# Gate and up projections of a hybrid decoder layer: from feature-major tiles to token-major 2x2 block products with seven products in place of eight

## The chip, the cores and the metric

The kernel runs on one core of one Trainium2 chip. The metric is device time in microseconds (us) of one execution. Before the change the median of three runs is 1140.72 us (1139.92 to 1142.09).

## The reference, cut to what matters

One decoder layer in float32, 256 tokens, model width 2048, feed-forward width 5632. The part that changes is the SwiGLU; the first residual, its norm and the down projection stand next to it.

```python
h = h + jnp.einsum('bse,ed->bsd', y, w_out[l])
u = rmsnorm(h, ln2_w[l])
ff = jax.nn.silu(jnp.einsum('bsd,df->bsf', u, w_ffn_gate[l])) * jnp.einsum('bsd,df->bsf', u, w_ffn_up[l])
h = h + jnp.einsum('bsf,fd->bsd', ff, w_ffn_down[l])
```

## The kernel before

Every large product is made of operands split into a high and a low part (`split`, L90: ScalarE copies the value to a rounded type, VectorE subtracts that copy from the value); high x high, high x low and low x high are summed in PSUM. Weights come from HBM in units of 128 x 2048 (class `Unit`, L94), two halves of 512 KB each, each issued on SyncE's queue into a `raw` tile (four slots) and split into `wh` and `wl` tiles (four slots each).

The work is a list, `program`, of steps: each has the unit it needs and a function that issues its matmuls. The loop at the end runs through it and issues loads three halves ahead of the step (`AHEAD`); `defer` puts work off by a number of steps. A planner orders the instructions of each engine's queue by this order and by when they are ready; each engine works its queue in order.

Two layouts occur. Feature-major (`fm_tile`, L151, `mm_fm`, L128): a 128-column tile of weights is the stationary operand, and the activations of all 256 tokens, high and low part side by side, are the moving one: 512 columns against the weights' high part and 256 against the low part, for each of 16 contraction tiles. Token-major (`tm_block`, L166, `mm_tm`, L139): 128 tokens are the stationary operand and 512 columns of weights the moving one, three matmuls for each contraction tile.

The gate and up projections are feature-major: 44 tiles of gate and 44 of up in turn, 88 steps. Behind each pair `ffn_post` (L545) adds the halves of the PSUM banks (`halves`, L146), applies the norm's scale, the tanh and the products, on VectorE, ScalarE and, for one multiplication, GpSimd (L551), and splits the result into `ff`, already in the layout that the down projection takes as stationary operand. The down projection is token-major. Before them stands the output projection, whose `out_post` (L502) adds the residual and makes the split left operands `hh`, 16 tiles. `resid_tok` (L532) transposes the residual on TensorE (L536) during the gate and up projections.

Other lines that are spoken of: L442 and L443 (`head`, attention scores, matmuls on whole float32 operands), L480 and L484 (`group_norm_apply`, GpSimd), L378 to L383 (`lru_out`, VectorE and ScalarE), L84 (matmuls at the start that warm TensorE up), L574 (`down_post`, VectorE reads PSUM).

Of the kernel before, what the change touches and what calls it, by code (L numbers as in the profile page):

```python
# [25 lines left out]
# columns of the packed per-channel parameters  # L26
# [5 lines left out]
def tile_hymba_layer(ctx: ExitStack, tc: tile.TileContext, A: dict, out: bass.AP):  # L32
# [48 lines left out]
    # the tensor engine's clock rises while the first loads are under way  # L81
# [12 lines left out]
    class Unit:  # L94
        """[128, 2048] of weights in two halves: 16 tiles of 128 columns, or 4 of 512."""
# [23 lines left out]
        def part(self, k, w, c0, cw):  # L119
            """columns c0:c0+cw of the k-th tile of width w, both parts"""  # L120
            o = k * w + c0
            j, o = o // 1024, o % 1024
            return self.h[j][:, o : o + cw], self.l[j][:, o : o + cw]

    halfway = []  # work to put into the middle of the next feature-major tile
    program = []  # (units to have loaded, compute)

    def mm_fm(ps, wh, wl, hl, first, last):  # L128
        """feature-major: ps[:, :256] + ps[:, 256:] collects w.T @ a"""
        pe.matmul(ps, wh, hl, start=first, stop=False)  # L130
        pe.matmul(ps[:, :S], wl, hl[:, :S], start=False, stop=last)  # L131

    def mm_fm1(ps, wh, wl, hl, first, last):
        """feature-major: ps collects w.T @ a"""
# [4 lines left out]
    def mm_tm(ps, hl, t, wh, wl, first, last):  # L139
        """token-major: ps collects a[:, tokens of t].T @ w"""  # L140
        ah, al = hl[:, t * P : t * P + P], hl[:, S + t * P : S + t * P + P]
# [4 lines left out]
    def halves(ps, dst):  # L146
        """dst = ps[:, :256] + ps[:, 256:]"""
# [18 lines left out]
    def tm_block(units, acts, post, together=1, split=()):  # L166
        """the last `together` units make one step, token tile after token tile; the last token
        tile's columns may be cut into pieces, each with a bank of its own"""
# [3 lines left out]
        def mm(unit, i, k, piece):  # L172
# [3 lines left out]
            mm_tm(ps[piece][:, c0 : c0 + cw], acts[4 * i + k], t, wh, wl, first, last)  # L176
# [25 lines left out]
    # work put off by a number of program steps  # L202
# [16 lines left out]
    def rsqrt_small(dst, var, scale, n):  # L219
        """dst = 1 / sqrt(var * scale + EPS), one Newton step behind the table's root"""  # L220
# [5 lines left out]
        # r (1.5 - 0.5 v r^2)  # L226
# [5 lines left out]
    def rms_scale(sumsq, r_tok, r_bc, then=None):  # L232
        """sumsq [128, 256]: squares summed over the tiles, not yet over the partitions"""
# [22 lines left out]
    r2 = cpool.tile([P, S], F32, name="r2")  # L256
    sumsq = cpool.tile([P, 512], F32, name="sumsq")

# [24 lines left out]
    xc = [None] * 4  # convolved input, two channel tiles each  # L283
    tt = [None] * 4  # tanh(c r / 2)
# [15 lines left out]
    def lru_decay():  # L300
        """c2 = -4 log_sigmoid(lambda) = 4 (log1p(exp(-|l|)) + max(-l, 0))"""
# [4 lines left out]
        # exp(-w) = (1 - tanh(w/2)) / (1 + tanh(w/2)) at w = |l| / 8, then three squarings  # L306
# [6 lines left out]
        # log1p(z) = 2 atanh(z / (2 + z))  # L313
# [46 lines left out]
    def lru_scan(n):  # L360
        """a = (1-T)/(1+T), sqrt(1-a^2) = (s^2 + T) / (s (1+T)) with s = sqrt(T) and a Heron step"""
# [32 lines left out]
    vv = [None] * 4  # [t][block]  # L394
# [91 lines left out]
    def ret_y(h):  # L486
# [5 lines left out]
        g = gnh[:, h : h + 1]  # half of the weight: sg is twice the gate  # L492
# [7 lines left out]
    hh = [None] * KT  # L500

    def out_post(f, ps):  # L502
        x = xs(f)
        if f < KT - 2:
            t = tmp("op")
            halves(ps, t)
            v.tensor_tensor(out=x, in0=x, in1=t, op=ALU.add)
        else:
            v.tensor_tensor(out=x, in0=ps[:, :S], in1=x, op=ALU.add)
        hl = act_tile("h", F32R)  # L510
        act.activation(out=hl[:, :S], in_=x, func=AF.Copy, scale=col(C_LN2 + f))
        v.scalar_tensor_tensor(
            out=hl[:, S:], in0=x, scalar=col(C_LN2 + f), in1=hl[:, :S].bitcast(F32),
            op0=ALU.mult, op1=ALU.subtract,
        )
        hh[f] = hl
        sq = sumsq[:, :S] if f == 0 else tmp("sq")
# [4 lines left out]
    r2h = cpool.tile([P, S], F32, name="r2h")  # L522

    def norm2():
        def half():
            v.tensor_scalar(out=r2h, in0=r2, scalar1=0.5, scalar2=None, op0=ALU.mult)

        rms_scale(sumsq[:, :S], r2_tok, r2, half)
# [3 lines left out]
    def resid_tok(cb):  # L532
        ps = [aux("ht"), aux("ht")]
        for i in range(4):
            for t in range(2):
                pe.transpose(ps[t][:, i * P : i * P + P], xs(4 * cb + i)[:, t * P : t * P + P], ident)  # L536
        for t in range(2):
            htok[(cb, t)] = xpool.tile([P, 512], F32, tag="xh", name=nm("htok"))
            act.copy(out=htok[(cb, t)], in_=ps[t])

# [1 line left out]
    ff = [None] * FT  # L542
    gate_ps = {}

    def ffn_post(f, gps, ups):  # L545
        g, s, w = tmp("fg"), tmp("fs"), tmp("fu")
        halves(gps, g)
# [289 lines left out]
```

## Time and profile before

| | |
|---|---|
| median of the runs | 1140.72 us (1139.92 to 1142.09) |
| the profiled execution | span 1138.9 us; the median of the runs is 1.8 us more |
| TensorE, weight loads, VectorE | busy 1119.9, 981.6, 744.2 us |
| ScalarE, GpSimd | busy 567.5, 111.4 us |
| DMA | 214.86 MB, mean 189 GB/s |

The span runs from the first to the last instruction of the profiled execution. Matmuls are pipelined: their recorded durations overlap, so the distance from one start to the next is what one costs. PE is TensorE, PEld its weight loads, DVE VectorE, ACT ScalarE, POOL GpSimd, SP SyncE.

### The profile page before, as it was taken

Reading aid. Unit: us, or ns where it says so; the run is one execution under the profiler, and the core shown is the slowest. Engines: PE = TensorE matmul, PEld = TensorE weight load, DVE = VectorE, ACT = ScalarE, POOL = GpSimd, SP = SyncE. Lnnn points to the kernel's source line nnn. Section 1 sums busy time; section 2 is a strip of 40 time slices with the busy share of each in tenths; the row PEclk is TensorE's granted clock in tenths of the full one; section 3 lists DMA queues with packets and bytes.
Section 4 is the critical chain, followed back from the end, with each engine's and each line's share of the span. In section 5 each row is a group of like instructions: output and inputs, shape, how many; then the busy total and the mean of one; then the engine's idle time right before and its main releaser. Section 6 shows DMA issues by size and latency. Waiting matters only on the chain.

```text
span 1138.9 us, 16705 instructions
## 1 busy us (share of the span) xinstructions
PE 1119.9 (98%) x6418; PEld 981.6 (86%) x6418; DVE 744.2 (65%) x1092; ACT 567.5 (50%) x826; POOL 111.4 (10%) x126
## 2 busy tenths in 40 slices
PE   7999999999999999999999999999999999999996
PEld 7998888889888988888888888888888888888896
DVE  7797899658877666666666666666666544444544
ACT  7575544456555555455554445445444434343432
POOL 4022310004400000000000000000000000000100
PEclk9999999999999999999999999999999999999999
DMA  7755655645455566555556555655655665656652
GB/s 244 250 167 174 229 172 184 204 148 183 151 185 187 186 197 188 187 184 190 185 182 192 195 186 188 194 190 187 190 197 186 226 199 188 199 188 194 194 185 94
DMA packets 62224, 214.86 MB, mean 189 GB/s; under 512 B 7104, under 2 KB 7488, under 8 KB 62144
## 3 DMA queue, kind: packets, MB, share of 16 engines
q1 hardware_dynamic: 61344, 211.70, 57.6%
q0 software_dynamic: 512, 1.57, 0.4%
q8 instruction: 50, 0.82, 0.3%
q10 hardware_dynamic: 288, 0.52, 0.1%
q14 instruction: 30, 0.25, 0.1%
HBM read 211.67 MB, written 2.10 MB: 188 GB/s over the span
## 4 chain that ended last, share of the span: by engine, by line
PE 93%; POOL 2%; DMA 2%; DVE 1%; ACT 1%; issue 1%; SPq 0%; DVEq 0%; POOLq 0%
PE fm L130 38%; PE fm L131 19%; PE tm L143 10%; PE tm L144 10%; PE tm L142 10%; POOL o L480 2%; PE fm L135 1%; PE fm L136 1%; PE fm L137 1%; DMA x<-in_x 1%; DMA gw<-in_gates 1%; PE g L636 0%; PE ht L536 0%; PE sc L442 0%; DVE wl L92 0%
## 5 line engine op out<-in xcount | busy, mean ns | idle before, releaser
L92 DVE TENSOR_TENSOR wl<-raw,wh 128x1024 fp32r<-128x1024 f32 (+1 forms) x400 | 481.9, 1209 | 307.6 <-ACT wh L91 303.9
L91 ACT CAST wh<-raw 128x1024 fp32r<-128x1024 f32 (+1 forms) x400 | 411.4, 1034 | 487.6 <-issue 208.3
L130 PE MATMUL fm<-h,wh 128*128 128x512 f32 x1408 | 489.1, 394 | 0.0
L131 PE MATMUL fm<-h,wl 128*128 128x256 f32 x1408 | 390.3, 277 | 0.0
L130 PEld LDWEIGHTS fm<-h,wh 128*128 128x128 f32 x1408 | 264.0, 188 | 61.1
L131 PEld LDWEIGHTS fm<-h,wl 128*128 128x128 f32 x1408 | 264.4, 188 | 0.1
L143 PE MATMUL tm<-wl,ff 128*128 128x512 f32 (+1 forms) x396 | 144.5, 366 | 0.0
L142 PE MATMUL tm<-wh,ff 128*128 128x512 f32 (+1 forms) x396 | 144.4, 366 | 0.0
L144 PE MATMUL tm<-wh,ff 128*128 128x512 f32 (+1 forms) x396 | 144.1, 365 | 0.0
L130 PE MATMUL fm<-u,wh 128*128 128x512 f32 x256 | 90.7, 398 | 0.0
L551 POOL TENSOR_TENSOR fu<-fu,r2h 128x256 f32<-128x256 f32 x44 | 32.6, 742 | 560.6 <-DVE fu L149 560.6
L142 PEld LDWEIGHTS tm<-wh,ff 128*128 128x128 f32 x396 | 74.4, 188 | 12.5
L143 PEld LDWEIGHTS tm<-wl,ff 128*128 128x128 f32 x396 | 74.4, 188 | 12.1
L144 PEld LDWEIGHTS tm<-wh,ff 128*128 128x128 f32 x396 | 74.3, 188 | 12.0
L130 PE MATMUL fm<-y,wh 128*128 128x512 f32 x224 | 77.7, 394 | 0.0
L131 PE MATMUL fm<-u,wl 128*128 128x256 f32 x256 | 71.9, 281 | 0.0
L131 PE MATMUL fm<-y,wl 128*128 128x256 f32 x224 | 61.7, 278 | 0.0
L130 PEld LDWEIGHTS fm<-u,wh 128*128 128x128 f32 x256 | 48.1, 188 | 11.5
L135 PE MATMUL fm<-u,wh 128*128 128x256 f32 x192 | 54.8, 285 | 0.0
L136 PE MATMUL fm<-u,wh 128*128 128x256 f32 x192 | 54.6, 284 | 0.0
L137 PE MATMUL fm<-u,wl 128*128 128x256 f32 x192 | 54.4, 283 | 0.0
L143 PE MATMUL tm<-wl,u 128*128 128x512 f32 x128 | 50.1, 392 | 0.0
(191 smaller groups left out, 1164.2 us busy)
## 6 DMA issues: line engine op xcount, KB each, us to landing
raw<-in_w_gate SPq DMA_DIRECT2D x88, 512.0 KB, 3.7
raw<-in_w_up SPq DMA_DIRECT2D x88, 512.0 KB, 3.7
raw<-in_w_down SPq DMA_DIRECT2D x88, 512.0 KB, 4.4
raw<-in_w_out SPq DMA_DIRECT2D x32, 512.0 KB, 4.3
raw<-in_w_k SPq DMA_DIRECT2D x16, 512.0 KB, 3.8
raw<-in_w_q SPq DMA_DIRECT2D x16, 512.0 KB, 4.4
raw<-in_w_v SPq DMA_DIRECT2D x16, 512.0 KB, 3.7
raw<-in_w_rg SPq DMA_DIRECT2D x16, 512.0 KB, 4.5
```

Source lines behind the costliest of these rows:

```text
L91: act.copy(out=dst_h, in_=src)
L92: v.tensor_tensor(out=dst_l, in0=src, in1=dst_h.bitcast(F32), op=ALU.subtract)
L130: pe.matmul(ps, wh, hl, start=first, stop=False)
L131: pe.matmul(ps[:, :S], wl, hl[:, :S], start=False, stop=last)
L135: pe.matmul(ps, wh, hl[:, :S], start=first, stop=False)
L136: pe.matmul(ps, wh, hl[:, S:], start=False, stop=False)
L137: pe.matmul(ps, wl, hl[:, :S], start=False, stop=last)
L142: pe.matmul(ps, ah, wh, start=first, stop=False)
L143: pe.matmul(ps, ah, wl, start=False, stop=False)
L144: pe.matmul(ps, al, wh, start=False, stop=last)
L480: pool.tensor_scalar(out=o, in0=o, scalar1=mv[:, n, 0:1], scalar2=gr[:, n : n + 1], op0=ALU.subtract, op1=ALU.mult)
L551: pool.tensor_tensor(out=w, in0=w, in1=r2h, op=ALU.mult)
```

## The change

Gate and up are computed together, token-major, in 11 blocks of 512 columns. In a block the left operand is a 2x2 arrangement: two tiles of 128 tokens by two contraction tiles of 128 (a11, a12, a21, a22); the right one is two contraction tiles by (512 gate columns, 512 up columns): b11, b12 (gate and up of the first contraction tile) and b21, b22. Such a product of 2x2 blocks takes eight block products; here it takes seven (a Strassen-Winograd scheme), each with sums of blocks as operands, and their results are added and subtracted at the end of the block.

- `Left` makes, for each pair of contraction tiles, the sums of left blocks s1 to s4 once, behind the output projection, and splits them.
- `Quad` replaces `Unit`: it loads four weight blocks in two halves, makes the sums t1 to t4 on GpSimd (t4 in every second step on VectorE) and splits b11, b22, b21, t1 and t2: 2560 columns in place of 2048. t1 and t2 share one slot of `raw`, which has six slots now.
- `quad` issues five products of split operands (three matmuls of 512 columns each) and two of whole float32 operands (p7 and p4, one matmul call each), into seven PSUM banks that are kept for the eight steps of a block.
- `ffn_post` runs once a block: it joins the seven banks to gate and up for both token tiles, applies tanh and products with the norm's scale per token, and transposes the result on TensorE (`turn`, eight transposes a block, three and four steps later).
- `ff_split` splits the transposed tiles with the loads of the first down block; before, this stood in `ffn_post`.
- `norm2` no longer spreads the scale over columns, and `resid_tok` uses one bank at a time.

The diff, cut to its core:

```diff
-    apool = ctx.enter_context(tc.tile_pool(name="acts", bufs=58))
+    apool = ctx.enter_context(tc.tile_pool(name="acts", bufs=56))
...
-    rpool = ctx.enter_context(tc.tile_pool(name="raw", bufs=4))
+    rpool = ctx.enter_context(tc.tile_pool(name="raw", bufs=6))
...
+    hh = [None] * (KT // 2)
+    hf = [None]
+    class Left:
+        def __init__(self, i, f, before):
+            a11, a21, a12, a22 = (f[:, n * P : n * P + P] for n in range(4))
+            g = act_tile("s")
+            s1, s2, s4 = (g[:, n * P : n * P + P] for n in range(3))
+            self.h, self.l = act_tile("ah", F32R), act_tile("al", F32R)
+            self.s4 = before.s4 if before else act_tile("s4", F32R)
+            self.o = 2 * P if before else 0
+            self.n = tmp("an")
+            v.tensor_tensor(out=s1, in0=a22, in1=a21, op=ALU.subtract)
+            v.tensor_tensor(out=s2, in0=a11, in1=s1, op=ALU.add)
+            v.tensor_tensor(out=s4, in0=s2, in1=a12, op=ALU.subtract)
+            pool.tensor_tensor(out=self.n[:, P:], in0=a11, in1=a21, op=ALU.subtract)
+            pool.tensor_copy(out=self.n[:, :P], in_=a22)
+            both = f.rearrange("p (a b) -> p a b", b=2 * P)[:, :, :P]
+            h0, l0 = (t[:, : 2 * P].rearrange("p (a b) -> p a b", b=P) for t in (self.h, self.l))
+            act.copy(out=h0, in_=both)
+            v.tensor_tensor(out=l0, in0=both, in1=h0.bitcast(F32), op=ALU.subtract)
+            split(self.h[:, 2 * P :], self.l[:, 2 * P :], g[:, : 2 * P])
+            split(self.s4[:, self.o : self.o + P], self.s4[:, self.o + P : self.o + 2 * P], s4)
+        def parts(self, which):
+            if which == "s4":
+                return self.s4[:, self.o : self.o + P], self.s4[:, self.o + P : self.o + 2 * P]
+            n = ("a11", "a12", "s1", "s2").index(which) * P
+            return self.h[:, n : n + P], self.l[:, n : n + P]
+        def whole(self, which):
+            return self.n[:, :P] if which == "a22" else self.n[:, P:]
     def out_post(f, ps):
         x = xs(f)
         if f < KT - 2:
-            t = tmp("op")
+            t = act_tile("op")[:, :S]
             halves(ps, t)
             v.tensor_tensor(out=x, in0=x, in1=t, op=ALU.add)
         else:
             v.tensor_tensor(out=x, in0=ps[:, :S], in1=x, op=ALU.add)
-        hl = act_tile("h", F32R)
-        act.activation(out=hl[:, :S], in_=x, func=AF.Copy, scale=col(C_LN2 + f))
-        v.scalar_tensor_tensor(
-            out=hl[:, S:], in0=x, scalar=col(C_LN2 + f), in1=hl[:, :S].bitcast(F32),
-            op0=ALU.mult, op1=ALU.subtract,
-        )
-        hh[f] = hl
-        sq = sumsq[:, :S] if f == 0 else tmp("sq")
+        if f % 2 == 0:
+            hf[0] = act_tile("hf")
+        act.activation(out=hf[0][:, (f % 2) * S : (f % 2) * S + S], in_=x, func=AF.Copy, scale=col(C_LN2 + f))
+        if f % 2:
+            hh[f // 2] = Left(f // 2, hf[0], hh[f // 2 - 1] if f // 2 % 2 else None)
+        sq = sumsq[:, :S] if f == 0 else act_tile("sq")[:, :S]
         act.activation(out=sq, in_=x, func=AF.Square)
         if f:
             v.tensor_tensor(out=sumsq[:, :S], in0=sumsq[:, :S], in1=sq, op=ALU.add)
-    r2h = cpool.tile([P, S], F32, name="r2h")
+    r2_half = cpool.tile([P, 2], F32, name="r2_half")
+    r2_sq = cpool.tile([P, 2], F32, name="r2_sq")
...
+    NB = DFF // 512
+    ff = [None] * (FT // 2)
+    ffh = [None] * (FT // 2)
+    ffl = [None] * (FT // 2)
+    class Quad:
+        def __init__(self, j, i):
+            self.src, self.n = A["w_gu"][j * (KT // 2) + i], j * (KT // 2) + i
+        def load(self, half):
+            r = rpool.tile([P, 1024], F32, tag="raw", name=nm("raw"))
+            nc.sync.dma_start(out=r, in_=self.src[:, half * 1024 : half * 1024 + 1024])
+            if half == 0:
+                self.ra = r
+                return
+            b11, b12, b22, b21 = self.ra[:, :512], self.ra[:, 512:], r[:, :512], r[:, 512:]
+            tt = rpool.tile([P, 1024], F32, tag="raw", name=nm("t12"))
+            self.t3, self.t4 = act_tile("t3"), act_tile("t4")
+            t1, t2 = tt[:, :512], tt[:, 512:]
+            pool.tensor_tensor(out=t1, in0=b11, in1=b12, op=ALU.add)
+            pool.tensor_tensor(out=t2, in0=t1, in1=b22, op=ALU.add)
+            pool.tensor_tensor(out=self.t3, in0=b12, in1=b22, op=ALU.add)
+            self.b11 = act_tile("bh", F32R), act_tile("bl", F32R)
+            split(*self.b11, b11)
+            self.b2 = [wpool.tile([P, 1024], F32R, tag=g, name=nm(g)) for g in ("wh", "wl")]
+            split(*self.b2, r)
+            self.t12 = [wpool.tile([P, 1024], F32R, tag=g, name=nm(g)) for g in ("wh", "wl")]
+            split(*self.t12, tt)
+            (v if self.n % 2 else pool).tensor_tensor(out=self.t4, in0=t2, in1=b21, op=ALU.add)
+    def mm3(ps, a, b, first, last):
+        (ah, al), (bh, bl) = a, b
+        pe.matmul(ps, ah, bh, start=first, stop=False)
+        pe.matmul(ps, ah, bl, start=False, stop=False)
+        pe.matmul(ps, al, bh, start=False, stop=last)
+    def ffn_block(j):
+        ps = {}
+        def quad(q, i):
+            def run():
+                first, last = i == 0, i == KT // 2 - 1
+                if first:
+                    for p in ("p1", "p2", "p3", "p7"):
+                        ps[p] = bank(p)
+                    for p in ("p5", "p6", "p4"):
+                        ps[p] = aux(p)
+                a = hh[i]
+                low = lambda pair: [t[:, :512] for t in pair]
+                high = lambda pair: [t[:, 512:] for t in pair]
+                mm3(ps["p1"], a.parts("a11"), q.b11, first, last)
+                mm3(ps["p2"], a.parts("a12"), high(q.b2), first, last)
+                mm3(ps["p3"], a.parts("s4"), low(q.b2), first, last)
+                pe.matmul(ps["p7"], a.whole("s3"), q.t3, start=first, stop=last)
+                mm3(ps["p5"], a.parts("s1"), low(q.t12), first, last)
+                mm3(ps["p6"], a.parts("s2"), high(q.t12), first, last)
+                pe.matmul(ps["p4"], a.whole("a22"), q.t4, start=first, stop=last)
+                if last:
+                    ffn_post(j, ps)
+                if j == 0 and i == 0:
+                    norm2()
+                if j == 0 and i in (1, 3, 5, 7):
+                    resid_tok(i // 2)
+            return run
+        for i in range(KT // 2):
+            q = Quad(j, i)
+            program.append(([q], quad(q, i)))
+    def ffn_post(j, ps):
+        c1, c3, c7, c5, g0 = (act_tile(n) for n in ("c1", "c3", "c7", "c5", "g0"))
+        act.copy(out=c1, in_=ps["p1"])
+        v.tensor_tensor(out=g0, in0=ps["p2"], in1=c1, op=ALU.add)
+        act.copy(out=c3, in_=ps["p3"])
+        act.copy(out=c7, in_=ps["p7"])
+        act.copy(out=c5, in_=ps["p5"])
+        v.tensor_tensor(out=c1, in0=ps["p6"], in1=c1, op=ALU.subtract)
+        v.tensor_tensor(out=c7, in0=c1, in1=c7, op=ALU.subtract)
+        g1 = c7
+        u1 = c1
+        e = act_tile("e")
+        v.tensor_tensor(out=e, in0=c1, in1=c5, op=ALU.subtract)
+        v.tensor_tensor(out=u1, in0=c7, in1=c5, op=ALU.subtract)
+        v.tensor_tensor(out=g1, in0=ps["p4"], in1=c7, op=ALU.subtract)
+        u0 = e
+        v.tensor_tensor(out=u0, in0=e, in1=c3, op=ALU.subtract)
+        for t, (g, u, th) in enumerate(((g0, u0, c3), (g1, u1, c5))):
+            act.activation(out=th, in_=g, func=AF.Tanh, scale=r2_half[:, t : t + 1])
+            v.scalar_tensor_tensor(out=g, in0=th, scalar=1.0, in1=g, op0=ALU.add, op1=ALU.mult)
+            v.scalar_tensor_tensor(out=g, in0=u, scalar=r2_sq[:, t : t + 1], in1=g, op0=ALU.mult, op1=ALU.mult)
+        def turn(b):
+            pt = aux("ft")
+            for c in range(2):
+                for t, g in enumerate((g0, g1)):
+                    o = c * S + t * P
+                    pe.transpose(pt[:, o : o + P], g[:, (2 * b + c) * P : (2 * b + c) * P + P], ident)
+            ff[2 * j + b] = act_tile("ff")
+            act.copy(out=ff[2 * j + b], in_=pt)
+        defer(3, lambda: turn(0))
+        defer(4, lambda: turn(1))
+    def ff_split(p):
+        ffh[p], ffl[p] = act_tile("ffh", F32R), act_tile("ffl", F32R)
+        split(ffh[p], ffl[p], ff[p])
...
-    for f in range(FT):
-        def post_g(ps, f=f):
-            gate_ps[f] = ps
-            if f == 0:
-                norm2()
-        def post_u(ps, f=f):
-            ffn_post(f, gate_ps.pop(f), ps)
-            if f in (4, 8, 12, 16):
-                resid_tok(f // 4 - 1)
-        fm_tile(Unit(A["w_gate"][f]), hh, range(KT), post_g)
-        fm_tile(Unit(A["w_up"][f]), hh, range(KT), post_u)
+    for j in range(NB):
+        ffn_block(j)
     for cb in range(4):
         if cb == 0:
             program.append(([], load_fw))
+        units = [
+            Unit(A["w_down"][11 * cb + i], 1, (lambda k, i=i: ff_split(2 * i + k)) if cb == 0 else None)
+            for i in range(11)
+        ]
         tm_block(
-            [Unit(A["w_down"][11 * cb + i]) for i in range(11)], ff,
+            units, lambda k: (ffh[k // 2], ffl[k // 2], (k % 2) * S),
             lambda t, ps, c0, cw, cb=cb: down_post(cb, t, ps, c0, cw),
...
+def _quads(left, right, np):
+    k, n = left.shape
+    a, b = (w.reshape(k // 256, 2, P, n // 512, 512).transpose(3, 0, 1, 2, 4) for w in (left, right))
+    q = np.stack([a[:, :, 0], b[:, :, 0], b[:, :, 1], a[:, :, 1]], axis=3)
+    return q.reshape(n // 512 * (k // 256), P, 2048)
```

More of the change, by code (lines that the diff above doesn't have):

```diff
@@ L530, in tile_hymba_layer @@
     htok = {}
     def resid_tok(cb):
[L533 to L536, printed above, removed]
         for t in range(2):
+            ps = aux("ht")
+            for i in range(4):
+                pe.transpose(ps[:, i * P : i * P + P], xs(4 * cb + i)[:, t * P : t * P + P], ident)
             htok[(cb, t)] = xpool.tile([P, 512], F32, tag="xh", name=nm("htok"))
-            act.copy(out=htok[(cb, t)], in_=ps[t])
@@ L542, in tile_hymba_layer @@
[L542 to L547, printed above, removed]
-        v.tensor_tensor(out=g, in0=g, in1=r2, op=ALU.mult)
-        act.activation(out=s, in_=g, func=AF.Tanh, scale=0.5)
-        halves(ups, w)
-        pool.tensor_tensor(out=w, in0=w, in1=r2h, op=ALU.mult)
-        v.scalar_tensor_tensor(out=g, in0=s, scalar=1.0, in1=g, op0=ALU.add, op1=ALU.mult)
-        v.tensor_tensor(out=g, in0=g, in1=w, op=ALU.mult)
-        hl = act_tile("ff", F32R)
-        split(hl[:, :S], hl[:, S:], g)
-        ff[f] = hl
+            act.copy(out=htok[(cb, t)], in_=ps)
```

26 lines of the change are left out of this document (15 added, 11 removed).

## The prediction

> **What bounds the kernel now.** I read the page's first and fourth parts, then busy time by stage, then the matmuls of the stage that changes.
>
> ```profile
> PE 1119.9 (98%) x6418; PEld 981.6 (86%) x6418; DVE 744.2 (65%) x1092; ACT 567.5 (50%) x826; POOL 111.4 (10%) x126
> ...
> PE 93%; POOL 2%; DMA 2%; DVE 1%; ACT 1%; issue 1%; SPq 0%; DVEq 0%; POOLq 0%
> ```
>
> ```profile
> 296.00:408.00 112.00, 112.00 (x704) 100.55 (x703) 80.41 (x128) 63.35 (x103) 2.51 (x2) 1.00 0.55 180
> 896.00:1139.00 243.00, 233.64 (x1154) 198.29 (x1152) 112.38 (x112) 95.71 (x106) 11.04 (x8) 0.99 0.57 183
> 395.30:888.00 492.70, 492.70 (x2856) 431.24 (x2855) 311.16 (x450) 247.50 (x365) 31.88 (x43) 1.00 0.59 189
> ```
>
> The chain of waits is 93% TensorE. In the table by stretch (length, then busy time of PE, PEld, DVE, ACT, POOL) the last row is the gate and up projections, first matmul to last: 492.7 us, TensorE never idle, VectorE at 63%, GpSimd at 6%. That is 88 steps of 5.60 us. Anything that shortens TensorE's step is a gain only while every other engine's step stays below it; so I cost the new step on each.
>
> **TensorE.** Durations in the trace overlap, so I count from start to start.
>
> ```profile
> 600.31 0.39 PE L130 MATMUL fm<-h,wh 128*128 128x512 f32 x1
> 600.54 0.27 PE L131 MATMUL fm<-h,wl 128*128 128x256 f32 x1
> 600.66 0.40 PE L130 MATMUL fm<-h,wh 128*128 128x512 f32 x1
> ```
>
> ```profile
> 901.67 0.39 PE L142 MATMUL tm<-wh,ff 128*128 128x512 f32 x1
> ...
> 903.03 0.39 PE L142 MATMUL tm<-wh,ff 128*128 128x512 f32 x1
> ```
>
> ```profile
> 172.32 0.59 PE L442 MATMUL sc<-rope,rope 128*128 128x256 f32 x2
> 172.75 0.38 PE L443 MATMUL sc<-rope,rope 128*128 128x128 f32 x2
> ```
>
> ```profile
> 451.91 1.04 PE L536 MATMUL ht<-ident,x 128*128 128x128 f32 x8
> 452.70 0.47 PE L130 MATMUL fm<-h,wh 128*128 128x512 f32 x1
> 453.01 0.28 PE L131 MATMUL fm<-h,wl 128*128 128x256 f32 x1
> ```
>
> Now: a pair of 512 and 256 columns takes 0.35 us, 16 pairs a step, 5.6 us. After: the six matmuls from 901.67 to 903.03 take 1.36 us, so a split block product (three of 512 columns) takes 0.68, and five of them 3.40. A whole-fp32 product is two instructions: 0.43 us for 256 columns (172.32 to 172.75), so 0.86 for 512, and two of them 1.72. The 88 new transposes, one per step on average, cost 0.11 each: eight and the matmul behind them take 1.10 (451.91 to 453.01), of which 0.23 is that matmul's. The whole product of 512 columns is the one price no row shows; it would have to be 2.0 us each, not 0.86, to reach the sum of the next part (3.40 + 0.11 + 2 x 2.05 = 7.6); below that it changes nothing, so I keep 0.86. Sum 5.23 us a step, 460 us for the stage, plus about 4 for the residual transposes and the norm as now: 464 against 493, 29 us less, if TensorE keeps the lead. Weight loads fall from 32 to 19 a step and stay beside the matmuls. The spread of the second norm's scale, two matmuls of 0.2 us, goes.
>
> **VectorE and GpSimd.** The four sums of weight blocks are new: t1, t2, t3 on GpSimd in each step, t4 on GpSimd in even steps and on VectorE in odd ones, all 128x512 with two SBUF inputs. The splits grow from 2048 to 2560 columns, on ScalarE (copy) and VectorE (subtract, two SBUF inputs). Do the two engines work at the same time? One place shows it, four GpSimd sums of just this size beside VectorE:
>
> ```profile
> 292.13 6.38 POOL L484 TENSOR_TENSOR o<-o,sg 128x512 f32<-128x512 f32 x4
> ```
>
> ```profile
> 291.88 1.22 DVE L92 TENSOR_TENSOR wl<-raw,wh 128x1024 fp32r<-128x1024 f32 x1 [0.22 <-ACT wh L91]
> 293.02 1.48 DVE L380 SCALAR_TENSOR_TENSOR q<-q,g 128x256 f32<-128x256 f32 x1
> 294.43 1.50 DVE L92 TENSOR_TENSOR y<-g,y 128x256 fp32r<-128x256 f32 x1
> 295.85 1.51 DVE L382 SCALAR_TENSOR_TENSOR g<-q,g 128x256 f32<-128x256 f32 x1
> 297.40 1.40 DVE L383 SCALAR_TENSOR_TENSOR g<-g,hs 128x256 f32<-128x256 f32 x1
> 298.72 1.21 DVE L92 TENSOR_TENSOR wl<-raw,wh 128x1024 fp32r<-128x1024 f32 x1
> ```
>
> ```profile
> 82.30 0.75 DVE L92 TENSOR_TENSOR xcs<-xc,xcs 128x256 fp32r<-128x256 f32 x2
> 82.97 0.28 DVE L350 TENSOR_SCALAR tt<-tt 128x256 f32<-128x256 f32 x1
> ```
>
> ```profile
> 280.36 1.23 DVE L92 TENSOR_TENSOR wl<-raw,wh 128x1024 fp32r<-128x1024 f32 x1 [0.22 <-ACT wh L91]
> 281.50 0.42 DVE L380 SCALAR_TENSOR_TENSOR q<-q,g 128x256 f32<-128x256 f32 x1
> ```
>
> ```profile
> 19.65 0.68 DVE L92 TENSOR_TENSOR wl<-raw,wh 128x512 fp32r<-128x512 f32 x1
> 20.25 0.15 DVE L320 SCALAR_TENSOR_TENSOR lam<-lam,lam 128x8 f32<-128x8 f32 x1
> ```
>
> VectorE's 256-column operations follow each other at 0.335 us when alone (two from 82.30 to 82.97), but at 1.425 us beside GpSimd ((298.72 - 293.02)/4). One GpSimd sum fits between two of them each time: they take turns, they do not overlap. A turn of GpSimd is 1.425 - 0.335 = 1.09 us. VectorE's own turns are 1.14 us for 1024 columns (280.36 to 281.50) and 0.60 for 512 (19.65 to 20.25). So the new step's turns add up:
> - even step: GpSimd 4 x 1.09 = 4.36; VectorE 0.60 + 1.14 + 1.14 = 2.88; together 7.24
> - odd step: 3 x 1.09 = 3.27; 2.88 + 0.60 = 3.48; together 6.75; mean of both 7.00
> - behind each block of eight steps, the part of the SwiGLU that has two SBUF inputs: four subtractions and four gate products of 512 columns, 8 x 0.60 = 4.8, or 0.60 a step.
>
> That is 7.60 us a step against TensorE's 5.23, so these turns become the bound: 88 x 7.60 = 669 us.
>
> Does every VectorE operation take turns?
>
> ```profile
> 278.05 4.71 POOL L480 TENSOR_SCALAR o<-o,mv,gr 128x128 f32<-128x128 f32 x3
> ```
>
> ```profile
> 279.35 0.43 DVE L378 TENSOR_TENSOR g<-fm,r 128x256 f32<-128x256 f32 x1 [0.23 <-PE fm L137]
> ```
>
> The multiplication that reads PSUM took 0.43 us in the middle of GpSimd's 4.71 us stretch; it did not wait. So the three operations of a block that read PSUM (g0, the first and the last subtraction) stay outside the sum.
>
> The Trainium skill, SBUF — State Buffer, section "SBUF: two separate sides", says the same in stricter form: VectorE operations with two SBUF inputs and GpSimd operations hold a shared pair of ports exclusively, for a whole instruction, and the loser waits. By that rule PSUM readers are free, as the trace agrees at 279.35; were they not, the sum would be some 20 us more by an estimate from the 512-column turn (33 x 0.60).
>
> An operation of 512 columns that reads PSUM costs VectorE 0.69 us:
>
> ```profile
> L574 DVE TENSOR_TENSOR htok<-tm,htok 128x512 f32<-128x512 f32 x7 | 4.8, 686 | 5.7 <-PE tm L144 5.7
> ```
>
> Lost between turns: the order is t1, t2, then ScalarE's copy of t1 and t2, then VectorE's subtraction. GpSimd has t3 and t4 to do during that copy, so a turn is used either way. At a block's end VectorE's three PSUM reads leave turns to GpSimd, which may by then be held by the buffers of the quad ahead (raw has six slots, three a quad). That costs from 0 to about 1.9 us a block (3 x 0.69); between those ends I take 1 us, 11 us in all, because GpSimd, with 3.8 us of turns a step, is about as far ahead as VectorE. Stage 669 + 11 = 680.
>
> **The rest, at nothing, with its cover.** ScalarE:
>
> ```profile
> L91 ACT CAST wh<-raw 128x1024 fp32r<-128x1024 f32 x384 | 402.2, 1051 | 485.0 <-issue 208.3 <-PE tm L144 158.7 <-PE fm L130 87.9
> L91 ACT CAST gh<-gw 128x512 fp32r<-128x512 f32 x4 | 2.5, 619 | 5.2 <-DMA gw<-in_gates 5.2
> ```
>
> It copies 0.62 + 2 x 1.05 = 2.7 us a step, and per block four evacuations, two tanh and two transposed copies, 8 x 0.62 / 8 = 0.6: 3.3 of 7.6. Its copy of t1, t2 waits for GpSimd; behind it queue the next quad's copies, and at a block's end the copy that frees p1's bank for TensorE's next block (seven of eight banks are in use, none doubled). TensorE has 2.4 us of slack a step for that. Were TensorE still the bound, a late copy would cost its lateness eleven times.
>
> ```profile
> raw<-in_w_gate SPq DMA_DIRECT2D x88, 512.0 KB, 3.7
> ```
>
> DMA: the same two 512 KB issues a step from SP, landing in 3.7 us. A slot is free again when the sums and splits that read it are done, one step before its next use. If it came later, the first sum would be late, for which TensorE, and not SP, pays. The output projection builds the left operands on VectorE (three sums of 128 columns and three splits per pair of tiles, in place of two subtractions) and GpSimd: VectorE is busy 80 of 112 us there. The down projection's first block splits 22 tiles of ff: 22 x 0.6 = 13 us in a stage where VectorE is busy 112 of 243. Both stay behind TensorE; without that cover each would cost its own few us.
>
> **Sum.** 680 - 493 = 187 us more on an execution whose span is 1138.9 us: 1326 us of span. The median of the runs shown, 1140.7, lies 1.8 us above that span, and I keep these: 1328 us.
>
> **Rivals.**
> 1. *Faster: TensorE keeps the lead.* One mechanism: GpSimd runs beside VectorE. Then a step is 5.23 us and the time 1140.7 - 29 = 1112. GpSimd alone would do 4 x 1.09 = 4.4 us at most. It decides below 5.23 us of turns a step. For it: in most of this trace GpSimd is idle, so the evidence is one stretch and some collisions. Against it: four turns in a row at 1.42 us. Between the two, if operations half overlap, a step of about 6.4 gives 88 x 6.4 - 493 = 70 more, 1211.
> 2. *Slower still: waits inside the order.* If VectorE's block end stands ahead of the next quad's splits in its queue, it waits for TensorE's whole last step, 5 us, eleven times, and the splits behind it wait too; and if a turn goes unused in each step while t2 is copied (1.05 us), the step is 8.6. Together 88 x 8.6 + 55 - 493 = 319 more, 1460; either alone about 1380 to 1420. For it: one queue per engine. Against it: GpSimd has t3, t4 to fill the gap.
> 3. *TensorE's clock falls,* since it idles 2.4 us a step, and about 7 us at a block's end (VectorE's 8 x 0.60 + 3 x 0.69 = 6.9 us there with up to five GpSimd turns between, 12 us, less a TensorE step).
>
> ```profile
> 1.04 4.13 PE L84 MATMUL warm<-ones 128*128 128x128 f32 x18 [1.04 <-DVE eps_t L77]
> ```
>
> ```profile
> 10.80:27.00 16.20, 12.91 (x96) 11.60 (x95) 16.04 (x28) 14.65 (x31) 11.14 (x8) 1.00 0.76 267
> ```
>
> At the start 18 passes of 128 columns took 4.1 us, 0.22 each, twice the 0.11 of the 128-column ones later. At half rate a step is 10.5 us and the time 1140.7 + 88 x 10.5 - 493 = 1572. Against it: between 10.8 and 27 us TensorE is busy 80% and the granted clock is 1.00.
>
> The Trainium skill, TensorE: Matmul & The Clock Gate, section "The HAM clock gate", lets the clock fall to half after a wholly idle window of about 3.4 us; by that rule a step's gap of 2.4 us would not do it and a block's end could, for a step or so. No stretch of this trace has such a gap in mid-kernel.
>
> **How the numbers follow.** Turns as the bound, 7.2 to 8.2 us a step: 0.77. Rival 1: 0.06 in full, 0.05 in half. Rival 2: 0.09. Rival 3 throughout: 0.03. The likeliest's own range is 1285 (a GpSimd turn of 1.0 us and nothing lost: 88 x 7.28 = 641, which gives 1289) to 1380; the range given goes up to 1420, taking in rival 2's single cases, and leaves out rival 1, rival 2 in full and rival 3. Three runs lie within 0.2% of each other, which is what can be told from no change. Faster 0.06, same 0.01, slower 0.93.
>
> **What would show it.** Right: in the new stage TensorE idle about 30%, waiting for GpSimd's sums and VectorE's subtractions; GpSimd's 512-column sums well above 1.3 us each and VectorE's subtractions of 1024 columns well above 1.23, the two alternating; the stage near 680 us. TensorE's split products 0.68 us, whole ones 0.86. Wrong: subtractions at 1.23 us beside a busy GpSimd (rival 1), VectorE idle behind TensorE at block ends (rival 2), a granted clock near 0.5 (rival 3). The weakest term is the turn of 1.09 us, taken from four operations.

## The result, and the profile after

The changed kernel takes 1351.8 us (median of four runs, 1350.9 to 1352.6) against 1140.3 for the kernel before: the ratio is 1.185 (95% interval 1.1835 to 1.1869), 211 us more. The prediction was 1328 (1285 to 1420).

The profile page of the changed kernel shows busy time and share of each engine, the TensorE clock in 40 slices, and the chain of waits that ended last.

```profile
PE 1195.8 (89%) x5360; PEld 894.1 (66%) x5360; DVE 1098.2 (81%) x1134; ACT 619.6 (46%) x871; POOL 653.4 (48%) x406
...
PEclk9999999999999998988888989998888999999999
...
PE 43%; DVE 32%; issue 12%; DMA 5%; POOL 5%; ACT 2%; SPq 0%; DVEq 0%; ACTq 0%; POOLq 0%
```

TensorE's part of the chain fell from 93% to 43%; VectorE's rose from 1% to 32%. The stage itself, by stretch (length, then busy time of PE, PEld, DVE, ACT, POOL, then clock, DMA share and rate):

```profile
395.00:1094.90 699.90, 564.78 (x1790) 340.00 (x1788) 638.21 (x443) 282.42 (x366) 557.27 (x304) 0.91 0.40 134
```

It takes 700 us from the first gate and up matmul to the first one of the down projection, where it was 493: 207 of the 211 us. The other 4 lie behind it: from the first down matmul to the end of the span it is 254.8 us, where it was 250.9. Two engines with "busy" of 638 and 557 of 700 us look as if they worked side by side. The rows from the middle of a block say otherwise; first GpSimd, then VectorE (start, duration):

```profile
701.19 2.26 POOL L605 TENSOR_TENSOR t<-t,raw 128x512 f32<-128x512 f32 x1
703.42 1.73 POOL L604 TENSOR_TENSOR t<-raw 128x512 f32<-128x512 f32 x1
705.10 1.72 POOL L606 TENSOR_TENSOR t<-raw,raw 128x512 f32<-128x512 f32 x1
706.78 2.27 POOL L605 TENSOR_TENSOR t<-t,raw 128x512 f32<-128x512 f32 x1
```

```profile
700.01 2.30 DVE L92 TENSOR_TENSOR wl<-raw,wh 128x1024 fp32r<-128x1024 f32 x1
702.23 1.77 DVE L92 TENSOR_TENSOR bl<-raw,bh 128x512 fp32r<-128x512 f32 x1
703.93 1.77 DVE L613 TENSOR_TENSOR t<-t,raw 128x512 f32<-128x512 f32 x1
705.62 2.29 DVE L92 TENSOR_TENSOR wl<-t,wh 128x1024 fp32r<-128x1024 f32 x1
```

They alternate one for one. Read from one VectorE start to the next, a 1024-column subtraction and a GpSimd sum take 2.22 us together (700.01 to 702.23; the prediction's turns give 1.14 + 1.09 = 2.23), a 512-column one and a sum 1.70 (702.23 to 703.93; 0.60 + 1.09 = 1.69). A third to two thirds of each "duration" is waiting for the other's turn. An operation of the block's end that reads PSUM, in the view of one line (minimum, median, maximum ns):

```profile
L658 DVE TENSOR_TENSOR g<-p,c x11: 677/678/682, 457.2 to 1096.3; 128x512 f32<-128x512 f32 x11
```

All eleven took 0.68 us, ten of them in the middle of a GpSimd sum: it does not wait. The 22 operations of the two other lines that read PSUM took 0.68 to 0.69 us.

So the steady state is as predicted. The excess of 20 us over the predicted 680 is, but for 4 us at the start of the down projection, in the work that follows a block's end. Here is one such place, about 38 us (five steps) behind the start of the block's first bank copy, where its transposes come: VectorE, ScalarE, GpSimd, and the issue of loads on SyncE.

```profile
678.53 1.21 DVE L92 TENSOR_TENSOR wl<-t,wh 128x1024 fp32r<-128x1024 f32 x1
679.67 0.68 DVE L92 TENSOR_TENSOR bl<-raw,bh 128x512 fp32r<-128x512 f32 x1
680.27 0.68 DVE L613 TENSOR_TENSOR t<-t,raw 128x512 f32<-128x512 f32 x1
684.37 1.75 DVE L92 TENSOR_TENSOR bl<-raw,bh 128x512 fp32r<-128x512 f32 x1 [3.42 <-ACT bh L91]
```

```profile
677.39 0.59 ACT L684 COPY ff<-ft 128x512 f32<-128x512 f32 x1 [4.37 <-PE ft L682]
677.87 0.62 ACT L91 CAST bh<-raw 128x512 fp32r<-128x512 f32 x1
```

```profile
675.81 1.72 POOL L613 TENSOR_TENSOR t<-t,raw 128x512 f32<-128x512 f32 x1
684.29 1.27 POOL L604 TENSOR_TENSOR t<-raw 128x512 f32<-128x512 f32 x1 [6.76 <-DMA raw<-in_w_gu]
```

```profile
680.41 0.90 SPq L596 DMA_DIRECT2D raw<-in_w_gu  x2
```

GpSimd stands for 6.8 us and VectorE for 3.4, so nobody uses the turn. Over the whole stage, neither of the two is at work for 30 us, by the rows of their timelines. Read backwards: GpSimd's sum t1 waits for a load; that load was issued at 680.41, when the last reader of its raw slot was done, VectorE's half of the split of an earlier b11 (679.67, 0.68 us); ahead of that stands ScalarE's half (677.87); and in ScalarE's queue that stands behind the copy of the transposed tiles, which waited 4.4 us for TensorE's transposes. VectorE's own 3.4 us are the same chain once more: it waits for the b11 copy at 683.71, which stands behind the second copy of transposed tiles (683.23, a wait of 4.7 us). Totals from the list of waits (us, times, longest):

```profile
POOL t L604 <- DMA raw<-in_w_gu: 92.7, 25, 7.5
...
ACT ff L684 <- PE ft L682: 79.8, 19, 7.2
```

The clock falls in the same place: by stretch, with the clock third from the right,

```profile
664.00:671.00 7.00, 5.80 (x23) 3.48 (x21) 7.00 (x7) 3.76 (x4) 5.00 (x4) 1.00 0.49 171
671.00:674.70 3.70, 0.66 (x3) 0.23 (x3) 3.70 (x3) 1.04 (x1) 3.70 (x3) 1.00 0.00 0
674.70:676.50 1.80, 1.24 (x5) 0.72 (x5) 1.80 (x3) 0.00 (x0) 1.80 (x2) 0.89 0.00 0
676.50:683.00 6.50, 6.04 (x18) 4.45 (x18) 4.45 (x4) 1.10 (x2) 1.03 (x1) 0.50 0.18 55
683.00:690.00 7.00, 7.00 (x24) 4.12 (x23) 5.15 (x4) 3.17 (x5) 5.38 (x4) 1.00 0.65 228
```

The half-rate stretch lies ahead of the second copy: the matmuls before its transposes follow each other at 0.42 us, where 0.23 was usual.

```profile
681.39 0.63 PE L618 MATMUL p<-wl,ah 128*128 128x512 f32 x1
681.81 0.63 PE L619 MATMUL p<-wh,al 128*128 128x512 f32 x1
```

### The profile page after: what moved, and what is told of

It is laid out like the page before. It is cut to its first block, busy times and chain, and to the rows that moved or that the text cites. A ratio compares the mean times of both kernels' runs of the same rounds, so it can differ in the third digit from the quotient of the medians.

```text
span 1349.7 us, 15178 instructions
## 1 busy us (share of the span) xinstructions
PE 1195.8 (89%) x5360; PEld 894.1 (66%) x5360; DVE 1098.2 (81%) x1134; ACT 619.6 (46%) x871; POOL 653.4 (48%) x406
## 4 chain that ended last, share of the span: by engine, by line
PE 43%; DVE 32%; issue 12%; DMA 5%; POOL 5%; ACT 2%; SPq 0%; DVEq 0%; ACTq 0%; POOLq 0%
DVE wl L92 14%; PE tm L146 8%; PE tm L147 8%; PE tm L148 8%; PE fm L130 8%; DVE bl L92 6%; PE fm L131 4%; DMA raw<-in_w_gu 4%; DVE t L613 3%; POOL o L483 2%; ACT wh L91 1%; DVE e L667 1%; DVE c L674 1%; DVE g L675 1%; POOL t L606 1%
## 5 line engine op out<-in xcount | busy, mean ns | idle before, releaser
L604 POOL TENSOR_TENSOR t<-raw 128x512 f32<-128x512 f32 x88 | 154.0, 1750 | 123.2 <-DMA raw<-in_w_gu 92.7
L618 PE MATMUL p<-wl,ah 128*128 128x512 f32 x264 | 133.6, 506 | 72.6 <-DVE wl L92 71.4
L605 POOL TENSOR_TENSOR t<-t,raw 128x512 f32<-128x512 f32 x88 | 173.2, 1968 | 13.5 <-DMA raw<-in_w_gu 12.5
L92 DVE TENSOR_TENSOR wl<-t,wh 128x1024 fp32r<-128x1024 f32 x88 | 172.3, 1958 | 0.6 <-ACT wh L91 0.6
L606 POOL TENSOR_TENSOR t<-raw,raw 128x512 f32<-128x512 f32 x88 | 160.9, 1833 | 0.5 <-DMA raw<-in_w_gu 0.2
L617 PE MATMUL p<-wh,ah 128*128 128x512 f32 x264 | 138.8, 577 | 20.5 <-ACT wh L91 20.0
L146 PE MATMUL tm<-wh,ffh 128*128 128x512 f32 (+1 forms) x396 | 145.0, 368 | 5.0 <-ACT c L657 3.5
L147 PE MATMUL tm<-wl,ffh 128*128 128x512 f32 (+1 forms) x396 | 145.3, 368 | 0.0
L148 PE MATMUL tm<-wh,ffl 128*128 128x512 f32 (+1 forms) x396 | 144.1, 367 | 0.0
L641 PE MATMUL p<-t,an 128*128 128x512 f32 x176 | 92.9, 609 | 19.1 <-DVE t L613 18.6
L617 PEld LDWEIGHTS p<-wh,ah 128*128 128x128 f32 x264 | 54.4, 213 | 71.0 <-ACT wh L91 40.1
L638 PE MATMUL p<-t,an 128*128 128x512 f32 x176 | 93.3, 613 | 1.0 <-POOL t L606 1.0
L613 POOL TENSOR_TENSOR t<-t,raw 128x512 f32<-128x512 f32 x44 | 84.7, 1925 | 0.0
```

Source lines behind the costliest of these rows:

```text
L92: v.tensor_tensor(out=dst_l, in0=src, in1=dst_h.bitcast(F32), op=ALU.subtract)
L146: pe.matmul(ps, ah, wh, start=first, stop=False)
L147: pe.matmul(ps, ah, wl, start=False, stop=False)
L148: pe.matmul(ps, al, wh, start=False, stop=last)
L604: pool.tensor_tensor(out=t1, in0=b11, in1=b12, op=ALU.add)
L605: pool.tensor_tensor(out=t2, in0=t1, in1=b22, op=ALU.add)
```

## The experiments

Stage lengths below run from the start of the stage's first matmul to the start of its last: 696 us in the changed kernel (to the down projection's first it is 700, as above). The turns sum to 669, so 27 us, 2.5 a block, are lost. Where a time below comes without a ratio, it is that of a single execution; with a ratio, it is the median of 4 to 10.

**All sums on VectorE.**

```diff
-            pool.tensor_tensor(out=t1, in0=b11, in1=b12, op=ALU.add)
-            pool.tensor_tensor(out=t2, in0=t1, in1=b22, op=ALU.add)
-            pool.tensor_tensor(out=self.t3, in0=b12, in1=b22, op=ALU.add)
+            v.tensor_tensor(out=t1, in0=b11, in1=b12, op=ALU.add)
+            v.tensor_tensor(out=t2, in0=t1, in1=b22, op=ALU.add)
+            v.tensor_tensor(out=self.t3, in0=b12, in1=b22, op=ALU.add)
...
-            (v if self.n % 2 else pool).tensor_tensor(out=self.t4, in0=t2, in1=b21, op=ALU.add)
+            v.tensor_tensor(out=self.t4, in0=t2, in1=b21, op=ALU.add)
```

> The changed kernel with all four sums of weight blocks on VectorE, none on GpSimd. Theory (turns: GpSimd's sums and VectorE's operations with two SBUF inputs exclude each other, a GpSimd turn of 512 columns costs 1.09 us and the same sum on VectorE 0.60): the step is VectorE's alone, 2.88 + 4 x 0.60 + 0.86 behind the blocks = 6.14 us, the stage 540 to 560, the time 1185 to 1215 us. Rival (the loss is in the raw slots and in the seven banks that are not doubled): slots and banks are used as before, the time stays above 1300 us.

1225.6 us, ratio 1.075 (1.0716 to 1.0776), stage 571. Giving VectorE 2 us more work a step made the kernel 126 us faster. The groups of VectorE's operations (busy, mean ns), first of the changed kernel, then of this one:

```profile
L92 DVE TENSOR_TENSOR wl<-t,wh 128x1024 fp32r<-128x1024 f32 x88 | 172.3, 1958 | 0.6 <-ACT wh L91 0.6
```

```profile
L92 DVE TENSOR_TENSOR wl<-t,wh 128x1024 fp32r<-128x1024 f32 x88 | 107.6, 1223 | 0.0
...
L604 DVE TENSOR_TENSOR t<-raw 128x512 f32<-128x512 f32 x88 | 60.6, 689 | 12.8 <-DMA raw<-in_w_gu 12.7
```

The same subtraction is back at 1.22 us. The slots-and-banks rival, which put the time above 1300, falls. The time is above my 1185 to 1215: 571 against 88 x 6.14 = 540. VectorE stands idle for about 36 us of the stage, most of it in the third, fifth and sixth step behind a block's end, where it waits for loads or for ScalarE's copies: the loss behind block ends once more, now without GpSimd.

**No sums.** All four sums removed; raw blocks take their place.

```diff
-            self.t3, self.t4 = act_tile("t3"), act_tile("t4")
+            self.t3, self.t4 = b12, b21
-            split(*self.t12, tt)
+            split(*self.t12, self.ra)
```

> The four sums of weight blocks left out: raw weight blocks stand in for them, with the same splits and the same matmuls, so the result isn't the reference's. Theory (turns): no GpSimd work in the step, VectorE 3.7 us, TensorE bounds at 5.23 us a step, stage about 464, time 1105 to 1130 us. Rival (whole float32 products dearer than 0.86 us, or banks that are not doubled): a step of 6 us or more, time above 1180 us.

1116.5 us, stage 467. Its stretch, and two whole products on TensorE:

```profile
395.00:862.00 467.00, 467.00 (x1787) 325.06 (x1786) 336.57 (x395) 280.65 (x367) 1.21 (x1) 1.00 0.59 198
```

```profile
700.85 1.02 PE L635 MATMUL p<-raw,an 128*128 128x512 f32 x2
701.71 1.02 PE L632 MATMUL p<-raw,an 128*128 128x512 f32 x2
```

TensorE is busy throughout, at 88 x 5.23 = 460 plus 4 as predicted, and a whole product costs 0.86 us (700.85 to 701.71). The saved product is real: 24 us, if the sums cost nothing. With them the kernel takes 235 us more. This run alone does not say why, since t1 and t2 no longer take up raw slots either; the run before it, with slots as they were, does.

**One more GpSimd sum a step.**

```diff
+    junk = cpool.tile([P, 512], F32, name="junkp")
...
+            self.t3x = junk
+            pool.tensor_tensor(out=self.t3x, in0=b12, in1=b22, op=ALU.add)
```

> The changed kernel with one more GpSimd sum of 512 columns in each step, t3 once more into a scratch tile that nobody reads. Theory (turns): one more turn of 1.09 us a step, 88 x 1.09 = 96 us more, 1435 to 1460 us. Rival (GpSimd has slack, as its own 3.5 x 1.25 = 4.4 us of an 8 us step would let one think): no change, 1345 to 1360 us.

1448.5 us, stage 793: 97 us more, 1.10 us for each of the 88 sums. GpSimd was idle for 143 of the 700 us (557 busy), and still an added sum costs its whole turn.

**t4 always on VectorE.**

```diff
-            (v if self.n % 2 else pool).tensor_tensor(out=self.t4, in0=t2, in1=b21, op=ALU.add)
+            v.tensor_tensor(out=self.t4, in0=t2, in1=b21, op=ALU.add)
```

> The changed kernel with the sum t4 on VectorE in every step, three sums left to GpSimd. Theory (turns): every second step gives up a GpSimd turn of 1.09 us for a VectorE turn of 0.60, 44 x 0.49 = 22 us less, 1325 to 1335 us. Rival (VectorE's own work is the bound and GpSimd's turns cost nothing more): 44 x 0.60 = 26 us more, about 1378 us.

1328.3 us, 23.5 less. VectorE got 44 more operations, and the stage fell by 19 us to 677, near the 22 that a GpSimd turn costs above VectorE's; most of the rest of the 23.5 is the start of the down projection, which came 0.6 us behind the last matmul here and 3.9 in the changed kernel.

**A GpSimd instruction that reads nothing.** First as a memset of a scratch tile:

```diff
+    junk = cpool.tile([P, 512], F32, name="junkp")
...
+            pool.memset(junk, 0.0)
```

> The changed kernel with one more GpSimd instruction of 512 columns in each step that reads nothing from SBUF, a memset of a scratch tile. If only GpSimd operations that read SBUF take turns with VectorE: at most 10 us more, 1350 to 1362 us. If every GpSimd operation takes a turn: 1.0 us a step or so, 1400 to 1450 us.

1351.8 us, which tells nothing: with no neighbour to hold it, the instruction left the stage. Its line (first and last start):

```profile
L609 POOL MEMSET junkp<- x88: 517/526/570, 0.8 to 76.1; 128x512 f32 x88
```

Then tied to its step, on the tile that the sum is about to write:

```diff
+            pool.memset(t1, 0.0)
             pool.tensor_tensor(out=t1, in0=b11, in1=b12, op=ALU.add)
```

> The changed kernel with a memset of t1's 512 columns on GpSimd just ahead of the sum that writes t1, so that it can't leave the step (in the run with a memset of a scratch tile, all 88 of them ran in the first 76 us, ahead of the stage). A memset reads nothing and takes 0.53 us there. If only GpSimd operations that read SBUF take turns with VectorE: it fills GpSimd's time while VectorE has the turn, 1345 to 1365 us. If every GpSimd operation takes a turn: 88 x 0.4 to 0.5 us, 1387 to 1400 us.

1339.3 us. GpSimd and VectorE of this run:

```profile
694.45 2.26 POOL L605 TENSOR_TENSOR t<-raw 128x512 f32<-128x512 f32 x1
696.65 0.52 POOL L604 MEMSET t<- 128x512 f32 x1
697.13 1.79 POOL L606 TENSOR_TENSOR t<-t,raw 128x512 f32<-128x512 f32 x1
```

```profile
695.49 2.30 DVE L92 TENSOR_TENSOR wl<-raw,wh 128x1024 fp32r<-128x1024 f32 x1
697.71 1.76 DVE L92 TENSOR_TENSOR bl<-raw,bh 128x512 fp32r<-128x512 f32 x1
```

The memset takes 0.52 us, begins the moment GpSimd's sum ends (694.45 + 2.26), while VectorE has its turn, and the pair's rhythm stays at 2.22 us (695.49 to 697.71). It takes no turn here. That the time even fell by 12 us isn't explained by that; the order of the queues behind block ends came out differently (GpSimd's wait for loads before t1, 92.7 us above, is 28.7 here). So the net price of a memset is not measured: the stage is 684 us, about 15 above the sum of the turns, and at most these 15 of the memsets' 88 x 0.52 = 46 us can be theirs.

The Trainium skill, SBUF — State Buffer, section "SBUF: two separate sides", counts against VectorE's two-input operations only those GpSimd operations that read SBUF. This run agrees at the rows shown: 0.52 us beside VectorE's turn, and the rhythm stays at 2.22.

**The block ends: slots or order?** Eight raw slots:

```diff
-    apool = ctx.enter_context(tc.tile_pool(name="acts", bufs=56))
+    apool = ctx.enter_context(tc.tile_pool(name="acts", bufs=52))
-    rpool = ctx.enter_context(tc.tile_pool(name="raw", bufs=6))
+    rpool = ctx.enter_context(tc.tile_pool(name="raw", bufs=8))
```

> The changed kernel with eight raw slots in place of six (and 52 act slots in place of 56, to make room). The stage took 700 us where the turns sum to 669, 2.8 us lost a block. Theory A (the loss is the wait of the loads for raw slots at the block's end): with one more pair of slots most of it goes, 1320 to 1335 us. Theory B (the loss lies in the order of ScalarE's queue, where the split of b11 stands behind the copy of the transposed tiles; slots only pass it on): part of it stays, 1335 to 1352 us.

1334.9 us, stage 676: on the border between the two theories. By the timelines, the time in which neither GpSimd nor VectorE works went from 30 to 6 us. Transposes later:

```diff
-        defer(3, lambda: turn(0))
-        defer(4, lambda: turn(1))
+        defer(6, lambda: turn(0))
+        defer(7, lambda: turn(1))
```

> The changed kernel with the transposes of a block put off by six and seven steps in place of three and four. Theory B (ScalarE's queue: copies of transposed tiles wait for TensorE, splits wait behind them): later, TensorE has caught up, so the copies don't wait, 1320 to 1340 us. Theory A (slots alone): no change, 1345 to 1358 us.

1325.0 us, stage 673, 4 us from the sum of the turns, with six slots; neither of the two engines works for 5 us. The wait of ScalarE's copies for the transposes, 79.8 us before, is no longer among the 60 longest. Its stretch and GpSimd's wait for loads:

```profile
396.50:1069.80 673.30, 549.16 (x1790) 348.40 (x1788) 627.40 (x441) 280.09 (x364) 543.15 (x304) 0.91 0.41 137
```

```profile
POOL t L604 <- DMA raw<-in_w_gu: 42.8, 16, 6.3
```

The mean clock is still 0.91 with the loss gone, so here the half-rate stretches cost next to nothing. In the changed kernel, where a copy waits for transposes behind half-rate matmuls, their part in the loss is not separated. The place of the transposes makes or removes the loss, and so does one more pair of slots: both are links of the chain, and breaking either one was enough here. That ScalarE's queue is the link which tips it is supported, not isolated: each such edit re-sorts all queues, as the memset showed.

**A version that wins?** TensorE and VectorE can be balanced: all sums on VectorE, and p1 as a third whole product, for 0.18 us more on TensorE and 0.60 less on VectorE. `Left` keeps a11 whole for it.

```diff
-            self.b11 = act_tile("bh", F32R), act_tile("bl", F32R)
-            split(*self.b11, b11)
+            self.b11 = b11
...
-                mm3(ps["p1"], a.parts("a11"), q.b11, first, last)
+                pe.matmul(ps["p1"], a.whole("a11"), q.b11, start=first, stop=last)
```

> All four sums on VectorE, and p1 as a third whole float32 product, so that b11 needs no split: TensorE 5.41 us a step, VectorE 2.28 + 2.40 + 0.86 = 5.54. Theory (VectorE's sum bounds, plus the loss at block ends that the run with all sums on VectorE showed, 574 - 540 = 34 us): stage 488 + 20 to 34, 1160 to 1180 us. Without the loss at block ends, which hung on the split of b11: 1140 us. Rival (it beats the kernel before): below 1136 us.

1177.7 us, ratio 1.033 (1.031 to 1.0346), stage 528 against 488: the loss is there though b11 has no split any more, so that split alone isn't its cause. VectorE's first sum of a step now waits for its load, once in each block, again about five steps behind the block's end:

```profile
DVE t L609 <- DMA raw<-in_w_gu: 24.7, 11, 2.6
```

With the late transposes as well:

> The version with all sums on VectorE and p1 as a third whole product, with the transposes six and seven steps later as well. Theory: VectorE's 5.54 us a step bounds, and the loss at block ends (528 - 488 = 40 us there) goes for the most part, as it did with the late transposes alone (700 to 673): stage 488 to 505, 1140 to 1158 us. Rival (late transposes help only where GpSimd stands in the chain): 1170 to 1180 us. It beats the kernel before only if the stage comes below 490 us.

1138.8 us, ratio 0.9992 (0.9983 to 1.0002): the same time as the kernel before, and 39 us less than with the transposes early. The stage is 488 us:

```profile
396.20:884.20 488.00, 485.15 (x1702) 308.46 (x1700) 481.80 (x654) 232.77 (x277) 0.74 (x2) 1.00 0.58 191
```

That this is VectorE's sum to the microsecond is partly luck: VectorE is idle for 6 us of it, and TensorE is busy for 485 (its own sum is 88 x 5.41 + 4 = 480). Both are close to their limit. With eight slots besides:

> The same with eight raw slots (and 52 act slots). Theory: loads wait less at the block's end, 0 to 10 us less than the version with six slots, 1138 to 1155 us. Rival (VectorE's sum alone bounds): the same time as with six slots.

1143.0 us, ratio 1.0037 (1.0024 to 1.005): no help. Last, with SiLU as one function on ScalarE, which spares two VectorE operations a block:

```diff
-            act.activation(out=th, in_=g, func=AF.Tanh, scale=r2_half[:, t : t + 1])
-            v.scalar_tensor_tensor(out=g, in0=th, scalar=1.0, in1=g, op0=ALU.add, op1=ALU.mult)
-            v.scalar_tensor_tensor(out=g, in0=u, scalar=r2_sq[:, t : t + 1], in1=g, op0=ALU.mult, op1=ALU.mult)
+            act.activation(out=th, in_=g, func=AF.Silu, scale=r2_tok[:, t : t + 1])
+            v.scalar_tensor_tensor(out=g, in0=u, scalar=r2_tok[:, t : t + 1], in1=th, op0=ALU.mult, op1=ALU.mult)
```

> The version with all sums on VectorE, p1 whole and late transposes, and SiLU taken by ScalarE as one function, so that each token tile needs one gate product on VectorE in place of two. VectorE: 5.54 - 2 x 0.60 / 8 = 5.39 us a step; TensorE 5.41. Theory (VectorE's sum bounds): stage 476 to 485 in place of 488, 1126 to 1136 us, faster than the kernel before by 0.3 to 1.2%. Rival (with both engines at 5.4 us a step waits between them eat the gain, or the table of another function is loaded anew for each block): 1138 us or more.

1131.5 us, ratio 0.9941 (0.9928 to 0.9955): 0.6% faster than the kernel before, a small difference, but the interval lies wholly below 1. Its stretch, and the one load of the function's table behind the first block:

```profile
393.90:876.90 483.00, 483.00 (x1701) 309.04 (x1700) 471.08 (x634) 234.16 (x278) 0.66 (x2) 1.00 0.58 195
```

```profile
L677 ACT ACT_TABLE_LOAD x1 | 1.3, 1283 | 1.0 <-DVE e L675 1.0
```

The time is as forecast, the theory isn't quite: TensorE has no idle time again, so it is TensorE that bounds (480 by its sum, 483 measured), not VectorE, which is 98% busy beside it. GpSimd does next to nothing, and the table is not loaded anew for each block. The SiLU edit was not run on the kernel before; it too has VectorE work there, but off the path.

## Why the prediction was right, point by point

- *TensorE's step of 5.23 us* held: 467 us where 464 was forecast, seen alone in the run without sums. A whole product cost the 0.86 that was extrapolated from 256 columns. The sign "TensorE idle about 30%" did not come: it was busy 565 of 700 us, idle 19%. A mean clock of 0.91 means about 120 us at half rate, which by an estimate adds at most 60 of the 101 us above 464; the rest is open (the view counts recorded durations, and the same matmul of line L617 has 0.39 to 1.41 us there).
- *Turns* held, in the rows and in three runs. One more GpSimd sum cost 1.10 us (1.09 predicted from four operations). t4 moved to VectorE gave back 23.5 us (22 expected), 19 of them in the stage. Moving all sums gave 126 us where GpSimd's 3.5 turns less VectorE's 3.5 sums make 88 x 3.5 x 0.49 = 151, less the VectorE time that no longer hides behind GpSimd's turns, 88 x 0.26 = 23: 128.
- *What reads PSUM is free of turns* held: 0.68 to 0.69 us, 33 times, nearly always beside a GpSimd sum.
- *Lost between turns, 1 us a block*, is the term that was mis-sized: 2.5 us a block to the last matmul, 27 us in place of 11. The place was named (slots at a block's end), the price was taken from VectorE's three PSUM reads. The chain in the trace is longer and begins with a step that I had costed at nothing: ScalarE's copies of the transposed tiles. I had put ScalarE at 3.3 of 7.6 us and seen that copies queue behind one that waits, but only behind the copy of t1 and t2; what counted was the split of b11 behind a copy that waits for transposes. Moving the transposes took 27 us away here and 39 in the version without b11's split.
- Between the last gate and up matmul and the first of the down projection TensorE stands for 3.5 us, until ScalarE's copy (L657) of the last block's p1 has freed a bank. I had named the seven undoubled banks and not put a price on the last block.

```profile
1094.92 0.50 PE L146 MATMUL tm<-wh,ffh 128*128 128x512 f32 x1 [3.48 <-ACT c L657]
```

- The 24 us above 1328 are thus 16 of loss between turns, 4 at the start of the down projection and 4 behind it, in a stage whose splits of ff I had put at nothing; what these last 4 consist of is open. The measured 1352 lies within the range that I gave to the turns alone, 1285 to 1380.
- *Rival 1* (TensorE keeps the lead) and its half form fell with the alternation. *Rival 2* had VectorE waiting for TensorE's last step; the order did bite, through ScalarE, and for about half that price (27 us of the 55). *Rival 3* occurred in part: a clock of 0.50 from 676.5 to 683, 0.91 on the mean over the stage. What the stretches cost is not separated from the 27 us.

## What to carry to other kernels

Work moved to an idle engine is only free if that engine doesn't exclude the busy one: where VectorE's operations have two inputs in SBUF and GpSimd's read SBUF too, as here, add their times and do not take the larger. Look in the trace for one place where both work, and read start to start; the busy columns count the waiting for a turn as work. And when a deferred copy waits in an in-order queue, price what stands behind it, not the copy.

## What was not expected of the hardware

The exclusion costs nothing extra: the two engines hand over within the rounding of the rows (2.22 us for 1.14 + 1.09), and with the transposes late the whole stage of 88 steps comes to 673 us where the turns sum to 669.

The half-rate stretches came without TensorE being idle for long at a time. In the one shown, the clock was 1.00 while TensorE was busy 0.66 of 3.70 us (671.00 to 674.70) and fell only after it had started again, at 674.76, with a longest gap of 3.1 us; it stayed at half for 6.5 us of nearly continuous work. The Trainium skill, TensorE: Matmul & The Clock Gate, section "The HAM clock gate", speaks of an idle window of about 3.4 us that runs free of the kernel; here no stretch of that length was wholly idle, and the clock fell all the same. The fall some time after the gap agrees with windows that run free of the work; what share of idle time is enough, these runs do not settle.
